# Two w_ada sections side by side: 512-wide adds on DVE, a quarter of the rows streamed through PE, rotary angles on POOL

## The chip, the cores and the metric

The kernel runs on one core of a Trainium2 chip. The metric is the device time of one execution in microseconds; shorter is better. Before the change it is 2480.28 us, the median of three runs (2477.94 to 2485.64).

The core's engines run side by side, each working through its own queue in order: PE (matrix multiply), DVE (vector), ACT (activation), POOL (GpSimd) and SP, which here only issues DMA transfers. An instruction that must wait holds up everything behind it in its engine's queue.

## The reference

One decoder block on x of 512 tokens by 2048 channels. A vector c gives six modulation vectors, and the first two of them (shift1, scale1) are needed before anything else can be projected:

```
mod = silu(c) @ w_ada + b_ada          # w_ada 2048 x 12288; six sections of 2048 columns
sh1, sc1, g1, sh2, sc2, g2 = split(mod)
u   = rmsnorm(x) * (1 + sc1) + sh1
z   = u @ w_in                         # q, k, v of two head groups, gates
y   = concat(rmsnorm(forgetting attention), rmsnorm(sparse attention)) @ w_out
h   = x + g1 * y
h   = h + g2 * swiglu(rmsnorm(h) * (1 + sc2) + sh2)
out = rmsnorm(h)
```

The sparse attention rotates q and k by cos and sin of position times frequency; the kernel makes these two tables itself.

## The kernel before, in words

Activations are held transposed, channels on the partitions: 16 chunks of 128 channels by 512 tokens. Every product with a weight is done in three passes of reduced-precision fp32r matmuls (high x high, low x high, high x low). For that each weight tile is split: ACT casts the high part `wh`, and DVE or POOL subtracts it to leave the low part `wl` (`fetch_w`, L218 to L243). `u` is split in the same way (`modulate_a` and `modulate_b`, L383 to L393: `mt` on DVE, `uh` on ACT, `ul` on DVE).

The change sits in the first stage, the loop of L474 to L545. It streams the first two sections of `w_ada` (scale1 and shift1, 33.5 MB), forms `silu(c) @ w_ada` as it goes, and feeds the first projections as soon as two chunks of `u` are known. It is written out by hand as steps; the order of the instructions in each queue is the order in which the steps emit them.

- A block `j` is 256 columns of both sections; there are `NJ` = 8 blocks of 8 steps. Each step loads one `w_ada` tile of 512 KB. The tiles go round in a ring of 8 buffers (tag `adw`), which the tiles of x, loaded first, use too.
- A tile before holds four row groups of 128 rows by 256 columns of one section. One step later, the row groups are multiplied with their scalar of `sl` (silu of c) and summed: DVE adds two or three of the four into `acc` (L492, L494); for the others ACT multiplies into `tm` (L499, L502) and POOL adds into `acc2` (L503).
- When a block is through (`due`, with the lags of `LAGS`), PE sums both accumulators over the partitions with a column of ones (L511), DVE adds the bias (L520) and makes `mt`, `uh` follows on ACT, and `ul` on DVE one step later.
- The two new chunks of `u` then release matmul units (`units`, L447), which are queued in `todo`; each step takes two of them, or three in the second half. A unit is three matmuls of 128x128 by 512. `S0` holds four banks for the query projection (first half) and then the compress inputs (second half), `S1` three banks for keys.
- The weights of these units are loaded in step 2 of each block (`w_pairs`, L437) and split one block later, in steps 0, 2 and 4 (L536 to L542): number 0 is the query or a compress tile, number 1 the key tile, number 2 (second half only) another compress tile. POOL makes the low parts; DVE makes that of number 1 in the second half.
- The rotary angles are a generator (`tables`, L397). From step 6 on it yields one DVE instruction per step (L543), 24 in all, and at its end two Sin passes on ACT.

After the loop, the key banks are rotated and the next projection begins (`z_qn`, L694).

The lines that the steps of the prediction touch:

```
due: step == n + LAGS[n == SLOTS - 1][what]        # LAGS = (3, 4, 5), (2, 3, 4)
units: for k in range(2) for m in range(len(outs)) # 8 units for S0, 6 for S1
for _ in range(2 if step < 8 * HJ + LAGS[0][2] else 3): todo.pop(0)()
```

Of the kernel before, what the change touches and what calls it, by code (L numbers as in the profile page):

```python
# [26 lines left out]
ADW = 8  # L27
# [50 lines left out]
def hymba_block(ctx: ExitStack, tc: tile.TileContext, x, c, positions, w_ada, b_ada, norm_attn,  # L78
                norm_ffn, w_in, b_fgate, cmp_pos, w_kc1, w_kc2, w_vc1, w_vc2, beta_fox, beta_nsa,
                w_out, w_gate, w_up, w_down, final_norm, cst, out):  # L80
    nc = tc.nc
    x, out = x[0], out[0]
    w_ada, w_in, w_out = w_ada[0], w_in[0], w_out[0]
# [25 lines left out]
    def bank(tag, shape=(P, T)):  # L109
        return ps.tile(list(shape), F32, tag=tag, name=uid("ps" + tag), bufs=SETS[tag])  # L110
# [16 lines left out]
    xtok = {}  # L127
    for t in range(NT):
        for g in range(2):
            xt = early.tile([P, D // 2], F32, tag="adw", name=uid("xtok"), bufs=ADW)  # L130
            nc.sync.dma_start(xt, x[t * P:(t + 1) * P, g * 1024:(g + 1) * 1024])
            xtok[t, g] = xt
    rows1 = early.tile([P, P], F32, name="rows1")
    nc.gpsimd.dma_start(rows1[0:96], b_ada.rearrange("o (r p) -> (o r) p", p=P))
# [7 lines left out]
    posi = early.tile([P, T], I32, name="posi")  # L142
# [4 lines left out]
    sl = con.tile([P, ND], F32, name="sl")  # L147
    se = con.tile([P, ND], F32, name="se")
    b = bank("o")
# [31 lines left out]
    tags = BANKS_A + BANKS_B  # L181
    for t in range(NT):
        for g in range(4):
            src = xtok[t, g // 2][:, g % 2 * T:(g % 2 + 1) * T]
            b = bank(tags[(t * 4 + g) % 8], (P, 4, P))
            for i in range(4):
                nc.tensor.transpose(b[:, i, :], src[:, i * P:(i + 1) * P], ident)
            dst = xT[:, 4 * g:4 * g + 4, t * P:(t + 1) * P]
            junk = early.tile([P, T], F32, tag="mt", name=uid("junk"), bufs=2)
            if g % 2 == 0:  # L190
                nc.scalar.activation(junk, src, AF.Square, accum_out=ssq4[:, t, g:g + 1])
                nc.vector.tensor_copy(dst, b)
            else:
                nc.vector.scalar_tensor_tensor(junk, src, 1.0, src, op0=OP.mult, op1=OP.mult,
                                               accum_out=ssq4[:, t, g:g + 1])
                nc.scalar.copy(dst, b)
    nc.vector.tensor_reduce(ssq, ssq4, axis=AX.X, op=OP.add)
    vec = con.tile([P, P + 64], F32, name="vec")
    b = bank("s")
    nc.tensor.transpose(b[:, 0:P], rows1, ident)  # L200
    nc.vector.tensor_copy(vec[:, 0:P], b[:, 0:P])
    b = bank("s")
# [192 lines left out]
    cosT = sinT = None  # L395

    def tables():  # L397
        nonlocal cosT, sinT
        cosT = wts.tile([P, T], F32, tag="cos", name="cosT")
        sinT = wts.tile([P, T], F32, tag="sin", name="sinT")  # L400
        ang = posi.bitcast(F32)
        nc.vector.tensor_copy(ang, posi)
        yield
        nc.vector.tensor_scalar(ang, ang, cs[:, K_FRQ:K_FRQ + 1], None, op0=OP.mult)
        yield
        for dst, turn in ((sinT, 0.0), (cosT, 0.25)):
            kk = mid.tile([P, T], F32, tag="wx", name=uid("kk"))
            nc.vector.tensor_scalar(kk, ang, 1.0 / TWO_PI, turn, op0=OP.mult, op1=OP.add)
            yield
            nc.vector.tensor_scalar(kk, kk, MAGIC, None, op0=OP.add)  # L410
            yield
            nc.vector.tensor_scalar(kk, kk, MAGIC, None, op0=OP.subtract)
            yield
            cur = ang
            for pc in _pi_parts():
                nc.vector.scalar_tensor_tensor(dst, kk, -pc, cur, op0=OP.mult, op1=OP.add)
                cur = dst
                yield
            if turn:
                nc.vector.tensor_scalar(dst, dst, TWO_PI / 4, None, op0=OP.add)  # L420
                yield
            nc.vector.tensor_scalar(dst, dst, PI_C, -PI_C, op0=OP.min, op1=OP.max)
            yield
        for dst in (sinT, cosT):
            nc.scalar.activation(dst, dst, AF.Sin)

    S0 = [bank(t) for t in BANKS_B]
    S1 = [bank("mm") for _ in range(3)]
# [6 lines left out]
    HJ = NJ // 2  # L435
# [25 lines left out]
    SLOTS = 8 * NJ  # L461
# [3 lines left out]
            if step == n + LAGS[n == SLOTS - 1][what]:  # L465
                return n

    def on_dve(n):
        return n % 2 == 0

    tiles, accs, accs2, sums, halves, fetched, todo = {}, {}, {}, {}, {}, {}, []
    extra_work = tables()
    step = 0
    while step < SLOTS + 8 or todo:  # L474
        j, r = divmod(step, 8)
        if j < NJ:
            sec, q0 = (1, 0)[r // 4], 4 * (r % 4)
            tiles[step] = early.tile([P, 4, 256], F32, tag="adw", name=uid("ad"), bufs=ADW)
            c0 = sec * D + j * 256
            nc.sync.dma_start(tiles[step], w_ada[:, c0:c0 + 256].rearrange("(q p) n -> p q n", p=P)[:, q0:q0 + 4, :])  # L480
        if r == 2 and j < NJ:
            fetched[j] = w_pairs(j)
        n = step - 1
        if 0 <= n < SLOTS:
            key, q0 = n // 4, 4 * (n % 4)
            if q0 == 0:
                accs[key] = early.tile([P, 256], F32, tag="acc", name=uid("acc"), bufs=3)
            acc = accs[key]
            for q in (0, 1, 3) if on_dve(n) else (0, 1):
                sc1 = sl[:, q0 + q:q0 + q + 1]  # L490
                if q0 + q == 0:
                    nc.vector.tensor_scalar(acc, tiles[n][:, q, :], sc1, None, op0=OP.mult)  # L492
                else:
                    nc.vector.scalar_tensor_tensor(acc, tiles[n][:, q, :], sc1, acc, op0=OP.mult, op1=OP.add)  # L494
            for q in (2,) if on_dve(n) else (2, 3):
                sc1 = sl[:, q0 + q:q0 + q + 1]
                if q0 + q == 2:
                    accs2[key] = early.tile([P, 256], F32, tag="acc2", name=uid("acc2"), bufs=3)
                    nc.scalar.activation(accs2[key], tiles[n][:, q, :], AF.Copy, scale=sc1)  # L499
                else:  # L500
                    tm = early.tile([P, 256], F32, tag="tm", name=uid("tm"), bufs=2)
                    nc.scalar.activation(tm, tiles[n][:, q, :], AF.Copy, scale=sc1)  # L502
                    nc.gpsimd.tensor_tensor(accs2[key], accs2[key], tm, op=OP.add)  # L503
        n = due(step, 0)
        if n is not None:
            jj = n // 8
            sums[jj] = bank("mm")
            for k2 in range(2):
                for av in (accs, accs2):
                    for i in range(2):  # L510
                        nc.tensor.matmul(sums[jj][:, 2 * k2 + i:2 * k2 + i + 1],  # L511
                                         av[2 * jj + k2][:, i * P:(i + 1) * P], one_col,
                                         start=k2 == 0 and av is accs and i == 0,
                                         stop=av is accs2, skip_group_check=True)
        n = due(step, 1)
        if n is not None:
            jj = n // 8
            for k2, sec in ((0, 1), (1, 0)):
                m0 = sec * ND + 2 * jj
                nc.vector.tensor_tensor(mod[:, m0:m0 + 2], sums[jj][:, 2 * k2:2 * k2 + 2], b_mod[:, m0:m0 + 2],  # L520
                                        op=OP.add)
            scale_vec(0, jj * 2, 2)
            pend = [modulate_a(0, i, xT[:, i, :], rstd1, early) for i in (2 * jj, 2 * jj + 1)]
        n = due(step, 2)
        if n is not None:
            u.extend([modulate_b(*h) for h in pend])
            jj = n // 8
            if jj < HJ:
                todo += units(halves[jj][0], jj, S0, ND // 2)
            if jj == HJ - 1:  # L530
                todo.append(keep_half)
            todo += units(halves[jj][1], jj, S1, ND)
        for _ in range(2 if step < 8 * HJ + LAGS[0][2] else 3):
            if todo:
                todo.pop(0)()
        if 0 < j <= NJ and r % 2 == 0 and r // 2 < len(fetched[j - 1]):  # L536
            i = r // 2
            w = fetched[j - 1][i](nc.vector if i == 1 and j > HJ else nc.gpsimd)
            halves.setdefault(j - 1, []).append(w)
            pr = 2 * (j - 1 - HJ) + i // 2  # L540
            if j > HJ and i != 1:
                todo += units(w, pr, S0, ND)  # L542
        if step >= 6:  # L543
            next(extra_work, None)
        step += 1  # L545
    for i in range(ND):
        nc.sync.dma_start(xsp[i], xT[:, i, :])
# [176 lines left out]
    b = bank("s")  # L724
    for t in range(NT):
        nc.tensor.matmul(b[0:8, t * P:], lf[:, t, :], tri[:, 0:T - t * P],
                         start=t == 0, stop=t == NT - 1)
# [196 lines left out]
    for pr in range(4):  # L924
# [4 lines left out]
        for i in range(2):  # L929
            q = pair("q", 6, "qf")  # L930
# [243 lines left out]
    kk = ExitStack()  # L1174
# [173 lines left out]
```

## Time and profile before

| | us |
|---|---|
| median of three runs | 2480.28 |
| the profiled execution | 2482.39 |
| its span in the trace | 2480.6 |
| PE busy | 2345.2 (95%) |
| DVE busy | 1626.7 (66%) |
| ACT busy | 1053.7 (42%) |
| POOL busy | 451.3 (18%) |

A trace row gives start, duration, engine, line, operation, the names of output and inputs and their shapes; in brackets stands how long the engine was idle before and what ended that. Matmuls overlap, so their pace is read from the distance of their starts. An fp32 matmul leaves two records, an fp32r matmul one. The granted clock of PE is a share of its full 2.4 GHz; it is at 1.00 or at 0.50 (1.2 GHz), and a stretch between has some of both.

### The profile page before, as it was taken

How to read it: one execution, taken by the hardware profiler on the slowest of the kernel's cores; microseconds unless marked ns; L12 is line 12 of the kernel's file. 1: busy time of each engine (PE TensorE's matmuls, PEld its weight loads, DVE VectorE, ACT ScalarE, POOL GpSimd, SP SyncE). 2: the span in 40 equal slices, each digit the busy share in tenths (PEclk: the TensorE clock that was granted, in tenths of full speed). 3: DMA queues.
4: the chain of work that ended last, by engine and by line, in shares of the span. 5: the costliest groups of instructions: out<-in, count | busy, mean ns of one | idle time of the engine just before them, and what ended most of it. 6: DMA issues, size and time to landing. Idle time of an engine off the chain costs nothing.

```text
span 2480.6 us, 38623 instructions
## 1 busy us (share of the span) xinstructions
PE 2345.2 (95%) x14659; PEld 2100.3 (85%) x14659; DVE 1626.7 (66%) x2757; ACT 1053.7 (42%) x1618; POOL 451.3 (18%) x466
## 2 busy tenths in 40 slices
PE   4688999999999989979999999999999899999998
PEld 3567888787887867779999999999999888888887
DVE  8995787877756566497677777777776633333333
ACT  4343543433423332255555555555555422222233
POOL 5564000200010221152121212121222100000011
PEclk7799999999999999989999999999999999999999
DMA  9783644444646257838988899888988654333322
GB/s 300 238 265 89 196 139 143 124 132 124 181 142 188 73 186 251 257 90 216 225 220 222 220 222 229 223 216 221 224 193 202 179 171 134 125 119 123 102 94 102
DMA packets 321690, 440.31 MB, mean 178 GB/s; under 512 B 25200, under 2 KB 216528, under 8 KB 321504
## 3 DMA queue, kind: packets, MB, share of 16 engines
q1 hardware_dynamic: 288080, 348.20, 43.6%
q0 software_dynamic: 31120, 85.45, 18.5%
q10 hardware_dynamic: 2304, 4.20, 0.4%
q8 instruction: 115, 1.88, 0.3%
q14 instruction: 71, 0.58, 0.1%
HBM read 340.18 MB, written 28.38 MB: 149 GB/s over the span
## 4 chain that ended last, share of the span: by engine, by line
PE 53%; DVE 1%; issue 0%; ACT 0%; DMA 0%; SPq 0%; DVEq 0%; ACTq 0%
PE py L1105 11%; PE py L1108 11%; PE py L1107 11%; PE psmm L255 3%; PE psmm L257 3%; PE psmm L256 3%; PE pss L255 2%; PE pss L256 2%; PE pss L257 2%; PE pso L257 1%; PE pso L256 1%; PE pso L255 1%; PE pso L1005 0%; DVE ul L1088 0%; DVE ls L1054 0%
## 5 line engine op out<-in xcount | busy, mean ns | idle before, releaser
L240 DVE TENSOR_TENSOR wl<-wr,wh 128x1024 fp32r<-128x1024 f32 (+2 forms) x194 | 218.5, 1126 | 359.6 <-ACT wh L239 358.0
L239 ACT CAST wh<-wr 128x1024 fp32r<-128x1024 f32 (+2 forms) x210 | 199.0, 948 | 498.1 <-PE psmm L256 205.5
L1108 PE MATMUL py<-uh,ls 128*128 128x256 f32 x1408 | 398.4, 283 | 3.7 <-DVE ls L1054 3.7
L1105 PE MATMUL py<-uh,hs 128*128 128x256 f32 x1408 | 399.4, 284 | 0.9 <-DVE ev L1122 0.5
L1107 PE MATMUL py<-ul,hs 128*128 128x256 f32 x1408 | 397.5, 282 | 2.5 <-DVE ul L1088 2.5
L1048 ACT CAST hs<-sum 128x1024 fp32r<-128x1024 f32 x176 | 184.7, 1049 | 379.6 <-PE py L1107 255.0
L1054 DVE TENSOR_TENSOR ls<-sum,hs 128x1024 fp32r<-128x1024 f32 x176 | 215.4, 1224 | 194.5 <-ACT hs L1048 194.5
L1107 PE MATMUL py<-ul,hx 128*128 128x256 f32 x1056 | 299.3, 283 | 4.0 <-DVE ul L1088 4.0
L1105 PE MATMUL py<-uh,hx 128*128 128x256 f32 x1056 | 299.0, 283 | 1.7 <-ACT uh L1087 1.4
L1108 PE MATMUL py<-uh,lx 128*128 128x256 f32 x1056 | 299.1, 283 | 0.0
L1108 PEld LDWEIGHTS py<-uh,ls 128*128 128x128 f32 x1408 | 266.8, 189 | 4.8 <-DVE ls L1054 4.7
L1107 PEld LDWEIGHTS py<-ul,hs 128*128 128x128 f32 x1408 | 266.7, 189 | 3.8 <-DVE ul L1088 3.8
L1105 PEld LDWEIGHTS py<-uh,hs 128*128 128x128 f32 x1408 | 267.5, 190 | 2.6 <-DVE ev L1122 1.3
L1044 POOL DMA_DIRECT2D lx<-raw x176 | 155.8, 885 | 592.5 <-ACT lx L1043 432.8
L1107 PEld LDWEIGHTS py<-ul,hx 128*128 128x128 f32 x1056 | 200.2, 190 | 5.3 <-DVE ul L1088 5.3
L1105 PEld LDWEIGHTS py<-uh,hx 128*128 128x128 f32 x1056 | 200.6, 190 | 2.2 <-ACT uh L1087 1.7
L1108 PEld LDWEIGHTS py<-uh,lx 128*128 128x128 f32 x1056 | 200.3, 190 | 0.0
L358 DVE SCALAR_TENSOR_TENSOR acc<-ad,sl,acc 128x512 f32<-128x512 f32 x180 | 143.0, 794 | 47.6 <-DMA ad<-in_w_ada_dram 45.9
L1043 ACT ACTIVATE lx<-raw 128x768 fp32r<-128x768 f32 x176 | 147.9, 840 | 1.8 <-DMA raw<-in_w_gate_dram 1.8
L1039 ACT CAST hx<-raw 128x768 fp32r<-128x768 f32 x176 | 144.3, 820 | 5.5 <-DMA raw<-in_w_gate_dram 5.5
L255 PE MATMUL psmm<-fh,wh 128*128 128x512 f32 x352 | 137.0, 389 | 0.0
L257 PE MATMUL psmm<-fh,wl 128*128 128x512 f32 x352 | 136.9, 389 | 0.0
(440 smaller groups left out, 5480.9 us busy)
## 6 DMA issues: line engine op xcount, KB each, us to landing
ad<-in_w_ada_dram SPq DMA_DIRECT2D x192, 512.0 KB, 4.6
lx<-raw POOLq DMA_DIRECT2D x176, 384.0 KB, 5.1
raw<-in_w_up_dram SPq DMA_DIRECT2D x176, 256.0 KB, 4.1
raw<-in_w_gate_dram SPq DMA_DIRECT2D x176, 256.0 KB, 4.5
wr<-in_w_down_dram SPq DMA_DIRECT2D x88, 512.0 KB, 3.6
wr<-in_w_in_dram SPq DMA_DIRECT2D x104, 256.0 KB, 3.5
wr<-in_w_in_dram SPq DMA_DIRECT2D x24, 512.0 KB, 4.4
wr<-in_w_out_dram SPq DMA_DIRECT2D x24, 512.0 KB, 5.1
```

What stands on the lines that cost most here:

```text
L239: nc.scalar.copy(wh[:, :, s], v)
L240: lo.tensor_tensor(wl[:, :, s], v, split_ap(wh)[:, :, s], op=OP.subtract)
L255: nc.tensor.matmul(dst, wh[:, k, w], ah, start=first, stop=False)
L256: nc.tensor.matmul(dst, wh[:, k, w], al, start=False, stop=False)
L257: nc.tensor.matmul(dst, wl[:, k, w], ah, start=False, stop=last)
L1043: nc.scalar.activation(lx[s], raw[s][:, 1:4, :], AF.Copy, scale=-1.0)
L1044: nc.gpsimd.dma_start(split_ap(lx[s]), raw[s][:, 1:4, :], accum_op=OP.add)
L1048: nc.scalar.copy(hs[s], sums[s])
L1054: nc.vector.tensor_tensor(ls[s], sums[s], split_ap(hs[s]), op=OP.subtract)
L1105: nc.tensor.matmul(o, wh[:, wi, js], vh[:, vi, :], start=k == 0 and j == 0, stop=False, skip_group_check=True)
L1107: nc.tensor.matmul(o, wh[:, wi, js], vl[:, vi, :], start=False, stop=False, skip_group_check=True)
L1108: nc.tensor.matmul(o, wl[:, wi, js], vh[:, vi, :], start=False, stop=k == KG - 1, skip_group_check=True)
```

## The change

A `w_ada` tile now holds two row groups of 128 rows by 512 columns: 256 of the scale section beside 256 of the shift section, brought by two transfers of 256 KB. A step therefore has two 512-wide row groups in place of four 256-wide ones. DVE adds both into `acc`, except in the steps that `on_pe` names (steps 0 to 6 of block 0, steps 3 to 6 of the others): there DVE adds the first, and one step later PE streams the second as an fp32 matmul, with the scalar broadcast to 128x128 as its weights, into one bank `rows`. After the last of these in a block, ACT copies one row of the bank (`row`). The sum over partitions takes this row and `acc`. ACT and POOL no longer multiply and add row groups.

The rotary angles go to POOL, all at once and ahead of the loop; ACT converts the positions for them, and the Sin passes stand at step 12. What was one fused instruction per part of 2 pi is now a multiplication and an addition. The low part of weight number 1 is made by DVE in all blocks. The tiles of x, which share the ring, change shape but not content.

```diff
+        ts, tt = nc.gpsimd.tensor_scalar, nc.gpsimd.tensor_tensor
         ang = posi.bitcast(F32)
-        nc.vector.tensor_copy(ang, posi)
-        yield
-        nc.vector.tensor_scalar(ang, ang, cs[:, K_FRQ:K_FRQ + 1], None, op0=OP.mult)
-        yield
+        nc.scalar.copy(ang, posi)
+        ts(ang, ang, cs[:, K_FRQ:K_FRQ + 1], None, op0=OP.mult)
+        kk = mid.tile([P, 2, T], F32, tag="wx", name=uid("kk"))
+        kt = kk[:, 1, :]
+        kk = kk[:, 0, :]
         for dst, turn in ((sinT, 0.0), (cosT, 0.25)):
...
+            ts(kk, ang, 1.0 / TWO_PI, turn, op0=OP.mult, op1=OP.add)
+            ts(kk, kk, MAGIC, None, op0=OP.add)
+            ts(kk, kk, MAGIC, None, op0=OP.subtract)
             cur = ang
             for pc in _pi_parts():
-                nc.vector.scalar_tensor_tensor(dst, kk, -pc, cur, op0=OP.mult, op1=OP.add)
+                ts(kt, kk, -pc, None, op0=OP.mult)
+                tt(dst, cur, kt, op=OP.add)
                 cur = dst
...
+                ts(dst, dst, TWO_PI / 4, None, op0=OP.add)
+            ts(dst, dst, PI_C, -PI_C, op0=OP.min, op1=OP.max)
...
-    def on_dve(n):
-        return n % 2 == 0
+    def on_pe(n):
+        j, r = divmod(n, 8)
+        return r < 7 if j == 0 else 3 <= r < 7
...
-    extra_work = tables()
+    tables()
...
-            sec, q0 = (1, 0)[r // 4], 4 * (r % 4)
-            tiles[step] = early.tile([P, 4, 256], F32, tag="adw", name=uid("ad"), bufs=ADW)
-            c0 = sec * D + j * 256
-            nc.sync.dma_start(tiles[step], w_ada[:, c0:c0 + 256].rearrange("(q p) n -> p q n", p=P)[:, q0:q0 + 4, :])
+            tiles[step] = early.tile([P, 2, T], F32, tag="adw", name=uid("ad"), bufs=ADW)
+            for i, sec in ((0, 1), (1, 0)):
+                c0 = sec * D + j * 256
+                nc.sync.dma_start(tiles[step][:, :, i * 256:(i + 1) * 256],
+                                  w_ada[:, c0:c0 + 256].rearrange("(q p) n -> p q n", p=P)[:, 2 * r:2 * r + 2, :])
...
-            for q in (0, 1, 3) if on_dve(n) else (0, 1):
+            for q in range(1 if on_pe(n) else 2):
...
-            for q in (2,) if on_dve(n) else (2, 3):
...
-                    nc.scalar.activation(tm, tiles[n][:, q, :], AF.Copy, scale=sc1)
-                    nc.gpsimd.tensor_tensor(accs2[key], accs2[key], tm, op=OP.add)
+        n = step - 2
+        if 0 <= n < SLOTS and on_pe(n):
+            jj, q = n // 8, 2 * (n % 8) + 1
+            first = n == 0 or not on_pe(n - 1)
+            if first:
+                rows[jj] = bank("mm")
+            nc.tensor.matmul(rows[jj], sl[:, q:q + 1].to_broadcast([P, P]), tiles[n][:, 1, :],
+                             start=first, stop=not on_pe(n + 1))
+            if not on_pe(n + 1):
+                row = early.tile([1, T], F32, tag="row", name=uid("row"), bufs=2)
+                nc.scalar.copy(row, rows[jj][0:1, :])
+                rows[jj] = row
...
+            for av, one in ((rows.pop(jj), one_col[0:1, :]), (accs.pop(jj), one_col)):
+                for i in range(4):
+                    nc.tensor.matmul(sums[jj][:, i:i + 1], av[:, i * P:(i + 1) * P], one,
+                                     start=one is not one_col and i == 0, stop=one is one_col,
+                                     skip_group_check=True)
...
-            w = fetched[j - 1][i](nc.vector if i == 1 and j > HJ else nc.gpsimd)
+            w = fetched[j - 1][i](nc.vector if i == 1 else nc.gpsimd)
...
-        if step >= 6:
-            next(extra_work, None)
+        if step == 12:
+            for dst in (sinT, cosT):
+                nc.scalar.activation(dst, dst, AF.Sin)
```

## Rows read from the trace of the kernel before

**Rows 1.** Busy us per stretch, PE, PEld, DVE, ACT, POOL, clock, DMA share, GB/s.

```profile
20.00:40.00 20.00, 4.32 (x17) 3.85 (x18) 18.01 (x34) 11.14 (x22) 12.86 (x14) 0.54 1.10 351
40.00:60.00 20.00, 11.48 (x38) 9.05 (x39) 19.57 (x28) 8.00 (x15) 12.30 (x11) 0.60 0.83 273
...
120.00:140.00 20.00, 18.70 (x86) 14.73 (x85) 19.45 (x30) 9.94 (x19) 10.18 (x12) 0.98 0.58 185
...
160.00:180.00 20.00, 17.16 (x82) 13.73 (x80) 19.41 (x26) 7.83 (x15) 12.78 (x12) 1.00 0.80 255
```

**Rows 2.** Waits of the DMA queue to 211 us: total, times, longest.

```profile
SPq L480 <- DVE acc L494: 61.9, 33, 5.5
```

**Rows 3.** DVE in order of time, from 20 us: start, duration.

```profile
22.72 3.61 DVE L494 SCALAR_TENSOR_TENSOR acc<-ad,sl,acc 128x256 f32<-128x256 f32 x7
```

**Rows 4.** Groups by line to 300 us: busy and mean, idle before.

```profile
L494 DVE SCALAR_TENSOR_TENSOR acc<-ad,sl,acc 128x256 f32<-128x256 f32 x144 | 111.1, 772 | 4.8 <-DMA ad<-in_w_ada_dram 0.6
...
L392 DVE SCALAR_TENSOR_TENSOR ul<-mt,mod,uh 128x512 fp32r<-128x512 f32 x16 | 17.7, 1146 | 0.0
```

**Rows 5.** PE in order of time, around the loop's end.

```profile
205.90 0.39 PE L255 MATMUL pss<-uh,wh 128*128 128x512 f32 x1
...
211.15 0.39 PE L257 MATMUL pso<-uh,wl 128*128 128x512 f32 x1
214.80 0.50 PE L255 MATMUL psmm<-uh,wh 128*128 128x512 f32 x1 [3.27 <-ACT wh L239]
```

**Rows 6.** DVE in order of time, 40 to 52 us.

```profile
43.36 0.42 DVE L410 TENSOR_SCALAR kk<-kk 128x512 f32<-128x512 f32 x1
...
46.39 0.22 DVE L520 TENSOR_TENSOR mod<-psmm,vec 128x2 f32<-128x2 f32 x2
...
46.85 1.41 DVE L386 SCALAR_TENSOR_TENSOR mt<-xT,a_vec,rstd 128x512 f32<-128x512 f32 x2
48.18 0.68 DVE L416 SCALAR_TENSOR_TENSOR sinT<-kk,posi 128x512 f32<-128x512 f32 x1
...
51.97 1.21 DVE L416 SCALAR_TENSOR_TENSOR sinT<-kk,sinT 128x512 f32<-128x512 f32 x1
```

**Rows 7.** The page's costliest groups.

```profile
L358 DVE SCALAR_TENSOR_TENSOR acc<-ad,sl,acc 128x512 f32<-128x512 f32 x180 | 143.0, 794 | 47.6 <-DMA ad<-in_w_ada_dram 45.9
```

**Rows 8.** The DMA queue's issues in order of time.

```profile
1.65 5.22 SPq L131 DMA_DIRECT2D xtok<-in_x_dram  x8
```

**Rows 9.** PE in order of time, fp32 matmuls: 172 us and 312 us.

```profile
172.47 1.84 PE L511 MATMUL psmm<-cs,acc 128*128 128x1 f32 x16
...
312.76 1.02 PE L726 MATMUL pss<-tri,lf 128*8 128x512 f32 x2
```

**Rows 10.** ACT in order of time, from 19 us.

```profile
24.59 0.59 ACT L175 COPY rstd<-psmm 128x512 f32<-128x512 f32 x1 [3.04 <-PE psmm L173]
```

**Rows 11.** POOL's groups by line and shape, whole span.

```profile
L503 POOL TENSOR_TENSOR acc<-acc,tm 128x256 f32<-128x256 f32 x80 | 68.5, 859 | 82.1 <-ACT tm L502 78.1
L240 POOL TENSOR_TENSOR wl<-wr,wh 128x1024 fp32r<-128x1024 f32 x12 | 31.3, 2608 | 6.8 <-ACT wh L239 6.8
L571 POOL TENSOR_TENSOR r<-r,sw 128x512 f32<-128x512 f32 x12 | 18.8, 1569 | 1.7 <-DVE r L569 0.8
...
L570 POOL TENSOR_TENSOR sw<-sw,sinT 128x512 f32<-128x512 f32 x12 | 16.2, 1348 | 88.6 <-ACT sw L568 65.7 <-DVE part L690 22.9
```

**Rows 12.** PE in order of time, the loop's first units.

```profile
50.97 0.80 PE L256 MATMUL pss<-ul,wh 128*128 128x512 f32 x1 [1.76 <-DVE ul L392]
...
55.83 0.41 PE L255 MATMUL pss<-uh,wh 128*128 128x512 f32 x1
```

**Rows 13.** A compress tile's cast on ACT, then PE's wait for it.

```profile
166.87 1.04 ACT L239 CAST wh<-wr 128x1024 fp32r<-128x1024 f32 x1
...
170.75 0.50 PE L257 MATMUL pss<-uh,wl 128*128 128x512 f32 x1 [0.94 <-POOL wl L240]
```

**Rows 14.** Busy us per stretch, columns as in group 1: a fall of the clock.

```profile
182.00:184.00 2.00, 2.00 (x6) 1.55 (x5) 1.97 (x3) 1.40 (x4) 2.00 (x2) 0.53 1.06 407
```

More of the change, by code (lines that the diff above doesn't have):

```diff
@@ L129, in hymba_block @@
         for g in range(2):
-            xt = early.tile([P, D // 2], F32, tag="adw", name=uid("xtok"), bufs=ADW)
-            nc.sync.dma_start(xt, x[t * P:(t + 1) * P, g * 1024:(g + 1) * 1024])
+            xt = early.tile([P, 2, T], F32, tag="adw", name=uid("xtok"), bufs=ADW)
+            nc.sync.dma_start(xt, x[t * P:(t + 1) * P, g * 1024:(g + 1) * 1024].rearrange("p (a b) -> p a b", b=T))
             xtok[t, g] = xt
@@ L183, in hymba_block @@
         for g in range(4):
-            src = xtok[t, g // 2][:, g % 2 * T:(g % 2 + 1) * T]
+            src = xtok[t, g // 2][:, g % 2, :]
             b = bank(tags[(t * 4 + g) % 8], (P, 4, P))
@@ L400, in tables @@
         sinT = wts.tile([P, T], F32, tag="sin", name="sinT")
+        ts, tt = nc.gpsimd.tensor_scalar, nc.gpsimd.tensor_tensor
         ang = posi.bitcast(F32)
-        nc.vector.tensor_copy(ang, posi)
-        yield
-        nc.vector.tensor_scalar(ang, ang, cs[:, K_FRQ:K_FRQ + 1], None, op0=OP.mult)
-        yield
-        for dst, turn in ((sinT, 0.0), (cosT, 0.25)):
[L407 to L413, printed above, removed]
+        nc.scalar.copy(ang, posi)
[3 more added lines that the diff above has]
+        kk = kk[:, 0, :]
+        for dst, turn in ((sinT, 0.0), (cosT, 0.25)):
+            ts(kk, ang, 1.0 / TWO_PI, turn, op0=OP.mult, op1=OP.add)
+            ts(kk, kk, MAGIC, None, op0=OP.add)
+            ts(kk, kk, MAGIC, None, op0=OP.subtract)
             cur = ang
             for pc in _pi_parts():
-                nc.vector.scalar_tensor_tensor(dst, kk, -pc, cur, op0=OP.mult, op1=OP.add)
+                ts(kt, kk, -pc, None, op0=OP.mult)
+                tt(dst, cur, kt, op=OP.add)
                 cur = dst
-                yield
             if turn:
[L420 to L425, printed above, removed]
+                ts(dst, dst, TWO_PI / 4, None, op0=OP.add)
+            ts(dst, dst, PI_C, -PI_C, op0=OP.min, op1=OP.max)
     S0 = [bank(t) for t in BANKS_B]
@@ L466, in due @@
                 return n
-    def on_dve(n):
-        return n % 2 == 0
-    tiles, accs, accs2, sums, halves, fetched, todo = {}, {}, {}, {}, {}, {}, []
-    extra_work = tables()
+    def on_pe(n):
+        j, r = divmod(n, 8)
+        return r < 7 if j == 0 else 3 <= r < 7
+    tiles, accs, rows, sums, halves, fetched, todo = {}, {}, {}, {}, {}, {}, []
+    tables()
     step = 0
@@ L484, in hymba_block @@
         if 0 <= n < SLOTS:
-            key, q0 = n // 4, 4 * (n % 4)
+            jj, q0 = n // 8, 2 * (n % 8)
             if q0 == 0:
-                accs[key] = early.tile([P, 256], F32, tag="acc", name=uid("acc"), bufs=3)
-            acc = accs[key]
-            for q in (0, 1, 3) if on_dve(n) else (0, 1):
+                accs[jj] = early.tile([P, T], F32, tag="acc", name=uid("acc"), bufs=2)
+            acc = accs[jj]
+            for q in range(1 if on_pe(n) else 2):
                 sc1 = sl[:, q0 + q:q0 + q + 1]
@@ L494, in hymba_block @@
                     nc.vector.scalar_tensor_tensor(acc, tiles[n][:, q, :], sc1, acc, op0=OP.mult, op1=OP.add)
-            for q in (2,) if on_dve(n) else (2, 3):
[L496 to L501, printed above, removed]
-                    nc.scalar.activation(tm, tiles[n][:, q, :], AF.Copy, scale=sc1)
-                    nc.gpsimd.tensor_tensor(accs2[key], accs2[key], tm, op=OP.add)
+        n = step - 2
[10 more added lines that the diff above has]
+                rows[jj] = row
         n = due(step, 0)
@@ L507, in hymba_block @@
             sums[jj] = bank("mm")
[L508 to L514, printed above, removed]
+            for av, one in ((rows.pop(jj), one_col[0:1, :]), (accs.pop(jj), one_col)):
[3 more added lines that the diff above has]
+                                     skip_group_check=True)
         n = due(step, 1)
```

## The prediction

> **What bounds the kernel now.** I read the page's engine shares first, and they put PE in front; but a share is a mean over stages, and the change touches only the first one. So I cut that stage into stretches of 20 us next. From 40 to 180 us DVE is busy over 19.4 us of every 20 (three of these seven stretches stand in the rows), while PE has 11 to 19, at granted clocks from 0.60 up to 1.00, and DMA falls from 351 GB/s to between 185 and 273 [rows 1]. The waits of the DMA queue say why it falls: 61.9 us in total for DVE's adds to free a tile [rows 2]. So DVE bounds the stage up to the last add. Its adds of 128x256 take 0.52 us each while POOL has nothing to do (seven in 3.61 us) [rows 3]; their mean over the stage is 0.77, x144 [rows 4]. Last I looked for where the stage hands over: the loop's last matmul starts at 211.15 and streams 0.23 us, so the loop ends on PE at 211.4; PE then stands until ACT has cast the next weight [rows 5]. What follows hangs on that end in the same way after the change, so I carry a shift of it through one to one.
>
> **What the change takes away.** DVE loses 160 adds of 256 columns and the 24 angle instructions, and gets 93 adds of 512. A 512-wide instruction with two tensors takes 0.68 us without POOL and 1.21 beside it [rows 6]; later in this kernel the same add has a mean of 0.79 [rows 7]. Per column block (8 steps) DVE then has 12 x 0.79 = 9.5, 1.9 for mod, scale and mt [rows 6], two ul of 1.15 [rows 4] and one weight subtraction, priced like an ul. That is 14.8 us; now 20 adds at 0.77 are 15.4 by themselves, with the rest and the angles beside them. DVE stops being the bound. The ACT and POOL adds go too, but neither engine was the bound, so I count nothing for them. The doubled number of w_ada transfers moves the same bytes in the same 1 KB runs; 20 issues per block at 0.65 us (eight in 5.22) [rows 8] are 13 us on the queue, under the pace found below: nothing.
>
> **What is late next: PE.** At full clock 23 matmuls start between 205.90 and 211.15, 0.228 us each [rows 5]. The loop has 432 of them: 18 per block for S1 (8 blocks), 24 for each of four first-half weight tiles, 24 for each of eight compress tiles. New are 35 fp32 matmuls of 512 columns. The trace has this form once: two records per matmul, the second 0.43 us after the first, so 0.86 us [rows 9]. Seven of them (block 0) run early, while PE has nothing else; 28 stand in PE's queue between the units. The column sums stay at 16 records per block, 1.84 us [rows 9].
>
> When can PE begin? Its first unit needs the low part of the first weight tile, which POOL subtracts, and all 26 angle instructions are now ahead of it in POOL's queue. They begin when ACT has converted the positions, behind the copy of rstd, which ends at 25.2 [rows 10]; plus 0.6 for a pass of 512 columns, 25.8. Eight of the 26 have two inputs: 1.35 and 1.57 us, mean 1.46, for 512 columns, 0.86 for 256 [rows 11]. The other 18 have one tensor input, and the trace has no such instruction on POOL. The two-input rows give 2.35 ns per column and 0.26 us fixed; half the slope gives 0.26 + 0.60 = 0.86. The ends: 0.42, what DVE takes for it [rows 6], and 1.57, the dearer two-input row. I take 0.86, as POOL must fetch half as much. Angles: 18 x 0.86 + 8 x 1.46 = 27.2, to 53.0; then the subtraction, 2.6 [rows 11]: PE starts in earnest at 55.6 (47.7 to 68.4). Before, its units ran on from 51.0 [rows 12], so they start later. ACT also stands in this time, since Sin waits for the angles; queued behind it are weight casts and a row copy needed only some 10 us later. The tiles come in meanwhile (19 of them and the weights are 18 MB, 52 us at 351 GB/s [rows 1]), so the DMA loses little.
>
> From there PE has 430 x 0.228 = 98.0, 28 x 0.86 = 24.1 and 7 x 1.84 = 12.9: 135.0 us. To this come its waits:
> - Blocks 1 to 3: from the column sums to the first ul. The rows have 46.39 for mod and 48.26 for the end of mt [rows 6], 1.87; one 512-wide add and one ul at 0.68 make 3.3, with the hand-over 3.4. Two units and one matmul (1.6) lie beside it: 1.8 each, 5.4. Later blocks have five units there: nothing.
> - Second half, a new wait: the row copy on ACT waits for the last streamed matmul of the block, and the cast of the next compress tile is queued behind it, then POOL's subtraction. 0.2 + 0.55 + 1.04 + 2.6 = 4.4 us [rows 10, 11, 13], beside two units and two matmuls (1.8): 2.5 in two blocks, 1.1 and 0.6 where more units lie between: 6.7. Before, this wait cost 0.94 [rows 13].
> - Clock: after a stand PE's matmuls came 0.43 us apart from 50.97 to 55.83, where the lower level ended [rows 12]; the same at the start here costs 2.5. One fall later, as from 182 (0.53 over 2 us) [rows 14], costs 0.9, and the two microseconds behind it as much again: 1.8.
>
> Sum: 55.6 + 135.0 + 5.4 + 6.7 + 2.5 + 1.8 = 207.0, against 211.4: 4.4 us less. By blocks: one of the first half has 42 x 0.228 + 3.4 + 1.8 + 1.8 = 16.6 us, one of the second 66 x 0.228 + 3.4 + 1.8 + 2.5 = 22.7; before, the loop took 160.4 from 51.0 on, 20 a block. The gain is made in the first half, and much of it is given back by the late start and in the second. The profiled execution took 2482.39 (span 2480.6), so 2478.0; it lay 2.1 above the median 2480.28, so against that 2475.9.
>
> In the Trainium skill, GPSIMD Engine Reference, section 4.1 Engine selection, POOL is about twice as slow as VectorE on two inputs and roughly at line rate on one. The trace agrees for two inputs (1.46 against 0.68); no run here shows one input. With one input at DVE's plain 0.68, the angles would end 3.2 us sooner and the time would be 2472.7.
>
> **Rivals.**
> 1. *PE's new waits stay hidden* (chance 0.31). The second half's 6.7 shrinks to the 0.9 per block seen before [rows 13], 3.6; the clock never falls again (1.8); one-input passes take 0.6, towards their lower end (4.7 off). 207.0 - 3.1 - 1.8 - 4.7 = 197.4: 2466. For it: the clock stayed at 0.98 and 1.00 in the later stretches though PE waited in each [rows 1]. Against: the row copy is ahead of the cast in ACT's queue.
> 2. *The stage falls to the DMA's pace* (0.07). 47 MB at 351 GB/s are 134 us, the last tile at 137; the last add stood 18 us before the loop's end, so about 160 and 2430. For it: the queue's waits [rows 2]. Against: the 135 us of PE work cannot begin at 25 us, and PE does not skip any of it.
> 3. *POOL's angles hold up the first units: slower* (0.21). One place: the first low part behind 26 instructions. If a one-input pass costs as much as the dearest two-input one, 1.57 [rows 11], the angles take 40.8 us with all 26 at that price, PE starts at 69.2, and the loop ends at 220.6: 9.2 us more, 2489.5. It decides from about 1.5 us per one-input pass. For it: these were 24 instructions of 0.42 to 1.21 us on DVE where rows show them [rows 6] and POOL has no row for them. Against: the read of one tensor less. The same page of the Trainium skill, in its opening, calls POOL the wrong choice for ordinary elementwise work, which speaks for this rival.
> 4. *The change doesn't do what it says* (part of the forecast): DVE is freed, but the time turns into PE's.
>
> **How the numbers follow.** A measurement of this kernel tells about 0.3%, 7.4 us, from no change. Forecast, -4.4 us: no change, chance 0.41; its own range is 2472 to 2483. Faster is rivals 1 and 2, 0.38. Slower is rival 3, 0.21. The unknown costs reach from -21 (one-input passes at 0.42, no new waits) to +19 (at 1.57, with two more falls of the clock and twice the new waits). I leave out rival 2 and the outer part of the others: 2462 to 2489.
>
> **What would show it.** PE's first unit with a low part near 55.6, right behind POOL's last angle and one subtraction; POOL's one-input passes near 0.86; streamed matmuls at 0.43 per record; DVE at about 65% from 60 to 200 us and waiting for PE's sums; PE busy over 90% there; in the second half PE waiting 2 to 3 us per block for a low part from POOL; the loop's last matmul near 207. A loop that ends before 200 or after 215 makes the prediction wrong, as would DMA at 350 GB/s throughout.

## The result, and the profile after

The changed kernel takes 2494.41 us, median of four runs (2491.69 to 2494.76), against 2480.07 for four of the kernel before (2477.94 to 2485.64). The ratio is 1.0052, with a 95% interval of 1.0034 to 1.0070. So it is slower, by some 13 us, and the interval leaves out no change; 2475.9 was predicted (range 2462 to 2489). The profiled executions took 2491.69 (span 2489.9) and 2482.39 (span 2480.6).

The stretches of [rows 1] and the one from 60 to 80 us, in the kernel after (same columns):

```profile
20.00:40.00 20.00, 13.36 (x40) 7.96 (x39) 14.31 (x25) 5.40 (x8) 12.93 (x9) 0.73 1.09 351
40.00:60.00 20.00, 1.59 (x2) 0.57 (x2) 19.09 (x21) 3.36 (x4) 18.98 (x13) 0.50 0.69 220
60.00:80.00 20.00, 11.92 (x34) 7.95 (x35) 0.00 (x0) 1.15 (x3) 7.68 (x6) 0.66 0.26 79
...
120.00:140.00 20.00, 17.06 (x66) 11.67 (x66) 13.77 (x21) 3.36 (x6) 2.25 (x1) 0.91 0.47 146
...
160.00:180.00 20.00, 18.08 (x81) 13.18 (x79) 12.67 (x16) 4.58 (x6) 5.26 (x2) 1.00 0.70 227
```

DVE is no longer the bound: from 120 to 140 and from 160 to 180 us it is busy 13 to 14 us of 20, where it had 19.4 in [rows 1]. But from 40 to 60 us PE does next to nothing, and from 60 to 80 DVE does nothing at all and the DMA moves 79 GB/s. POOL alone is full, up to 66 us. PE in order of time shows what that does to the loop's start and end (it answers to [rows 5, 12]; in brackets the idle time before and what ended it):

```profile
49.22 0.80 PE L256 MATMUL pss<-ul,wh 128*128 128x512 f32 x1 [1.14 <-DVE ul L392]
68.08 0.80 PE L257 MATMUL pss<-uh,wl 128*128 128x512 f32 x1 [18.06 <-POOL wl L240]
...
229.68 0.39 PE L257 MATMUL pso<-uh,wl 128*128 128x512 f32 x1
233.19 0.50 PE L255 MATMUL psmm<-uh,wh 128*128 128x512 f32 x1 [3.12 <-ACT wh L239]
```

The first low part comes at 68.08 instead of the 55.6 predicted, and the loop's last matmul at 229.68 instead of 207 (211.15 in [rows 5]): 18.5 us later than before. POOL's groups from 25 to 66 us, by shape (busy us, mean ns), say why the start is late:

```profile
L414 POOL TENSOR_SCALAR kk<-kk 128x512 f32<-128x512 f32 x8 | 13.9, 1735 | 0.7
L415 POOL TENSOR_TENSOR sinT<-sinT,kk 128x512 f32<-128x512 f32 x3 | 4.3, 1430 | 0.2
...
L410 POOL TENSOR_SCALAR kk<-kk 128x512 f32<-128x512 f32 x2 | 3.3, 1650 | 0.2
...
L409 POOL TENSOR_SCALAR kk<-posi 128x512 f32<-128x512 f32 x2 | 1.6, 816 | 0.2
...
L419 POOL TENSOR_SCALAR cosT<-cosT 128x512 f32<-128x512 f32 x1 | 0.6, 613 | 0.1
```

The passes with one operation (L410, L411, L414, L418) cost more than the two-input adds (L415); those with two operations (L409, L419) cost about half as much as the adds.

The rest of the loss is inside the loop. ACT's Sin, which waited for POOL's angles, was over at 66.4; what follows repeats in every later block. One block's hand-over, ACT and DVE first, then PE, 96 to 108 us:

```profile
97.92 0.57 ACT L501 COPY row<-psmm 1x512 f32<-1x512 f32 x1 [9.73 <-PE psmm L497]
98.41 1.78 ACT L239 CAST wh<-wr 128x1024 fp32r<-128x1024 f32 x2
...
100.22 2.49 DVE L240 TENSOR_TENSOR wl<-wr,wh 128x768 fp32r<-128x768 f32 x1 [4.22 <-ACT wh L239]
102.63 1.52 DVE L490 SCALAR_TENSOR_TENSOR acc<-ad,sl,acc 128x512 f32<-128x512 f32 x2
104.07 0.22 DVE L517 TENSOR_TENSOR mod<-psmm,vec 128x2 f32<-128x2 f32 x2
...
96.81 1.02 PE L497 MATMUL psmm<-ad,sl 128*128 128x512 f32 x2
...
97.90 0.40 PE L256 MATMUL psmm<-ul,wh 128*128 128x512 f32 x1
...
106.01 0.50 PE L255 MATMUL pss<-uh,wh 128*128 128x512 f32 x1 [1.91 <-ACT uh L388]
107.25 0.50 PE L256 MATMUL pss<-ul,wh 128*128 128x512 f32 x1 [0.73 <-DVE ul L392]
```

ACT waits for PE's last streamed matmul (L497) to copy its row; both casts are queued behind the copy; DVE's queue stands before the low part of the second weight, and behind that stand two adds of the next block, and then `mod` and `mt`. PE's sums over the partitions are over before (they start at 100.56). Only then comes `uh` on ACT, for which PE waits. So PE's own stream decides when PE gets its next `u`. I call this the tie. DVE's waits from 40 to 200 us (total, times, longest) sum it up:

```profile
DVE wl L240 <- ACT wh L239: 43.2, 6, 22.4
```

The longest is the stand at the start, 59.4 to 81.8 us. It has two parts, as ACT and then DVE show in order of time:

```profile
65.75 0.63 ACT L542 ACTIVATE cosT<-cosT 128x512 f32<-128x512 f32 x1 [15.56 <-POOL cosT L419]
79.48 0.57 ACT L501 COPY row<-psmm 1x512 f32<-1x512 f32 x1 [13.10 <-PE psmm L497]
81.77 2.50 DVE L240 TENSOR_TENSOR wl<-wr,wh 128x768 fp32r<-128x768 f32 x1 [22.36 <-ACT wh L239]
```

For the first 7 us ACT's queue stands in Sin for POOL. After that it stands 13.1 us in front of the row copy, while PE, late, works through the units queued ahead of its streamed matmuls. So the tie already makes the larger part of this stand; the other five waits, 20.8 us, are the tie alone.

### The profile page after: what moved, and what is told of

Read it like the earlier page. It is cut to its first block, busy times and chain, and to the rows that moved or that the text cites. A ratio compares the mean times of both kernels' runs of the same rounds, so it can differ in the third digit from the quotient of the medians.

```text
span 2489.9 us, 38545 instructions
## 1 busy us (share of the span) xinstructions
PE 2361.6 (95%) x14729; PEld 2099.8 (84%) x14729; DVE 1579.6 (63%) x2675; ACT 1015.7 (41%) x1531; POOL 407.9 (16%) x408
## 4 chain that ended last, share of the span: by engine, by line
PE 53%; DVE 1%; issue 1%; ACT 0%; DMA 0%; SPq 0%; DVEq 0%; ACTq 0%
PE py L1103 11%; PE py L1106 11%; PE py L1105 11%; PE psmm L257 3%; PE psmm L255 3%; PE psmm L256 3%; PE pss L255 2%; PE pss L257 2%; PE pss L256 2%; PE pso L257 1%; PE pso L256 1%; PE pso L255 1%; PE pso L1003 0%; DVE ul L1086 0%; DMA out_dram<-ot 0%
## 5 line engine op out<-in xcount | busy, mean ns | idle before, releaser
L240 DVE TENSOR_TENSOR wl<-wr,wh 128x1024 fp32r<-128x1024 f32 (+2 forms) x198 | 231.9, 1171 | 394.9 <-ACT wh L239 392.8
```

What stands on the lines that cost most here:

```text
L240: lo.tensor_tensor(wl[:, :, s], v, split_ap(wh)[:, :, s], op=OP.subtract)
```

## The experiments

Two theories at the start. A: the late start is the cause, made by the price of POOL's one-operation passes ahead of the first low part. B: PE is the bound, by the streamed matmuls and by waits for a cast behind the row copy, and the late start is absorbed. From the second set on, C: the tie, which turns an earlier start into longer waits; against D: the tiles (DVE's adds, the DMA) hold an early PE.

Ratios are against the kernel before, timed on the same chip. Its median was 2480.07 beside the kernel after, 2483.76 beside e1 to e4, 2482.18 beside f1 to f4 and 2484.11 beside g1 to g4; these differ by up to 0.16%, so smaller differences between ratios of two sets say nothing. "Loop end" is the start of the loop's last matmul, and the loop is counted from the first low part on PE; both are from one profiled execution of each kernel.

| kernel | first low part | loop end | PE idle in the loop | granted clock in the loop | ratio (95%) |
|---|---|---|---|---|---|
| before | 51.6 | 211.2 | 29.4 | 0.88 | 1 |
| after | 68.1 | 229.7 | 13.0 | 0.95 | 1.0052 (1.0034 to 1.0070) |
| e1 two operations | 60.0 | 226.3 | 15.8 | 0.94 | 1.0041 (1.0028 to 1.0054) |
| e2 late angles | 48.4 | 233.4 | 21.9 | 0.87 | 1.0023 (1.0009 to 1.0037) |
| e3 no stream | 68.4 | 207.9 | 21.0 | 0.92 | 0.9971 (0.9960 to 0.9982) |
| e4 cast first | 68.9 | 215.1 | 3.7 | 0.98 | 1.0006 (0.9995 to 1.0016) |
| f1 late, cast first | 46.8 | 196.8 | 5.5 | 0.96 | 0.9923 (0.9908 to 0.9939) |
| f2 f1, fewer streamed | 46.5 | 196.9 | 9.0 | 0.87 | 0.9928 (0.9913 to 0.9942) |
| f3 late, no stream | 48.9 | 199.9 | 30.3 | 0.89 | 0.9943 (0.9928 to 0.9959) |
| f4 f3, two edits more | 49.7 | 203.0 | 29.9 | 0.87 | 0.9950 (0.9935 to 0.9966) |
| g1 e1 and e4 | 60.0 | 206.3 | 3.7 | 0.98 | 0.9962 (0.9948 to 0.9975) |
| g2 f1, two operations | 46.9 | 196.7 | 5.4 | 0.96 | 0.9935 (0.9911 to 0.9959) |
| g3 f1, mixed | 46.2 | 193.0 | 7.0 | 0.95 | 0.9914 (0.9896 to 0.9932) |
| g4 f1, angles on DVE | 45.5 | 199.3 | 5.6 | 0.94 | 0.9921 (0.9900 to 0.9942) |

**e1: two operations per pass on POOL.**

```diff
-            ts(kk, kk, MAGIC, None, op0=OP.add)
+            ts(kk, kk, 1.0, MAGIC, op0=OP.mult, op1=OP.add)
...
-                ts(kt, kk, -pc, None, op0=OP.mult)
+                ts(kt, kk, -pc, 0.0, op0=OP.mult, op1=OP.add)
...
```

> The 13 POOL passes that have one operation and an immediate (1.49 to 2.08 us each in the changed kernel) are written with two operations (times 1.0, or plus 0.0), as the form of L409 that took 0.69 and 0.94; nothing else changes. Theory A (the late start of PE, made by the price of the one-operation passes): 13 x about 0.85 us go, POOL's angles end near 55 instead of 65.7, the first low part is there near 57 and PE's first unit with it stands near 57 instead of 68; the time falls by about 11 us, to 2483. Theory B (PE is the bound by the streamed matmuls and the waits for a cast behind the row copy; the late start is absorbed): the passes may get cheaper, but the time stays within 4 us of 2494.

POOL's groups of this kernel, as above, and the first low part on PE:

```profile
L414 POOL TENSOR_SCALAR kk<-kk 128x512 f32<-128x512 f32 x8 | 7.4, 928 | 0.7
...
L404 POOL TENSOR_SCALAR posi<-posi,cs 128x512 f32<-128x512 f32 x1 | 1.6, 1573 | 19.9 <-ACT posi L403 19.9
...
L410 POOL TENSOR_SCALAR kk<-kk 128x512 f32<-128x512 f32 x2 | 1.6, 776 | 0.2
```

```profile
59.98 0.79 PE L257 MATMUL pss<-uh,wl 128*128 128x512 f32 x1 [8.80 <-POOL wl L240]
```

The same arithmetic with a second, empty operation takes 0.93 us instead of 1.74; L404, left with one operation, still takes 1.57. So the form sets the price. PE starts 8 us earlier, yet the loop ends only 3.4 us earlier and the time is 2494.24: the same. Theory B was right that the time would not move, but the reason is in the next runs.

**e2: late angles.** The angles, in the changed kernel's forms, become a generator again, one POOL instruction per step from step 8 on, with Sin at its end.

```diff
-    tables()
+    extra_work = tables()
...
+        if step >= 8:
+            next(extra_work, None)
```

> The angles stay on POOL in the same forms, but are issued one per step from step 8 on, behind the first weight's low part in POOL's queue, with Sin at the end. Theory A: PE's first unit waits only for the first modulated tile and stands near 50 instead of 68; the loop ends near 212 instead of 230 and the time falls by about 18 us, to 2476, near the kernel before. Theory B: PE begins earlier but has the same 135 us of work and the same waits, and is overtaken by the tiles' arrival; the loop ends no more than 6 us earlier, the time is 2488 or above.

PE in order of time, around the starts of three blocks, then the whole loop with its granted clock (third from the right), then DVE's waits:

```profile
47.78 0.79 PE L256 MATMUL pss<-ul,wh 128*128 128x512 f32 x1 [1.80 <-DVE ul L392]
48.37 0.63 PE L257 MATMUL pss<-uh,wl 128*128 128x512 f32 x1
...
69.04 0.50 PE L255 MATMUL pss<-uh,wh 128*128 128x512 f32 x1 [3.13 <-ACT uh L388]
71.63 0.80 PE L256 MATMUL pss<-ul,wh 128*128 128x512 f32 x1 [2.10 <-DVE ul L392]
...
92.27 0.49 PE L255 MATMUL pss<-uh,wh 128*128 128x512 f32 x1 [2.50 <-ACT uh L388]
94.87 0.79 PE L256 MATMUL pss<-ul,wh 128*128 128x512 f32 x1 [2.10 <-DVE ul L392]
```

```profile
48.37:233.63 185.26, 163.38 (x599) 118.04 (x597) 114.88 (x142) 37.17 (x51) 62.52 (x34) 0.87 0.63 203
```

```profile
DVE wl L240 <- ACT wh L239: 33.6, 6, 9.8
```

PE starts 20 us earlier than after, and the loop ends no earlier. DVE waits 33.6 us for casts, now all through the loop. PE waits 4.3 to 5.2 us at each start of blocks 1 to 3 (the rows show the first two of these), and after the wait at 71.63 its matmuls come back 0.43 us apart instead of 0.23: a mean granted clock of 0.87, between the levels of 1.2 and 2.4 GHz, costs 0.13 x 185 = 24 us of the loop. The median, 2489.03 (2483.34 to 2501.90; the profiled execution is the slowest of these), is 5.4 us under the kernel after. Theory A's 18 us did not come; what B named "the same waits" did, but they grew.

**e3: no streamed matmuls after block 0.**

```diff
-        return r < 7 if j == 0 else 3 <= r < 7
+        return j == 0 and r < 7
...
```

> The 28 streamed fp32 matmuls of blocks 1 to 7 go back to DVE as 28 more adds of 512 columns (and with them the row copies and the first four column sums of these blocks); block 0 and the angles stay as they are. Theory B (PE bound by them): 28 x 0.86 = 24 us of PE and about 9 us of waits behind the row copy go; the loop's end falls from 230 to about 200, the time to about 2462. Theory A (late start): PE still begins at 68; DVE then has 16 x 0.79 + 5.3 = 18 us per block, under what the second half of PE needs, so what PE gains is about 8 to 12 us; the time is about 2483.

```profile
80.00:100.00 20.00, 14.39 (x57) 10.67 (x55) 19.50 (x28) 4.29 (x6) 2.57 (x1) 0.91 0.61 194
```

The time is 2477.50, between the two theories. The loop ends 21.8 us earlier than after, where B had 30, but the first low part stays at 68.36, and DVE is the bound again, with 19.50 of 20 us in this stretch. A and B each hold a part of the cost. With the streamed matmuls the row copies went too, and with them the tie: DVE's stand for the cast at the start is 4.42 us here, where after has 22.36, though the angles are as early and as slow.

**e4: the cast ahead of the row copy.** Only the place where ACT's copy is issued moves, behind the casts of the same step.

```diff
-            if not on_pe(n + 1):
-                row = early.tile([1, T], F32, tag="row", name=uid("row"), bufs=2)
-                nc.scalar.copy(row, rows[jj][0:1, :])
-                rows[jj] = row
...
+        n = step - 2
+        if 0 <= n < SLOTS and on_pe(n) and not on_pe(n + 1):
+            jj = n // 8
+            row = early.tile([1, T], F32, tag="row", name=uid("row"), bufs=2)
+            nc.scalar.copy(row, rows[jj][0:1, :])
+            rows[jj] = row
```

> Only ACT's order changes: the copy of the streamed row is issued behind the cast of the next block's first weight instead of ahead of it. Theory B: the second half's wait for POOL's low part (0.9 to 2.4 us per block on PE) goes and the time falls by about 6 us, to 2488; the rows of PE show no wait for POOL there. Theory A: the waits may go, but the time stays within 3 us of 2494, and PE's first unit with a low part stays at 68.

The same hand-over as shown above of after (ACT, DVE, PE), the whole loop, and DVE's waits:

```profile
96.18 0.58 ACT L540 COPY row<-psmm 1x512 f32<-1x512 f32 x1 [8.80 <-PE psmm L497]
96.66 0.83 ACT L239 CAST wh<-wr 128x768 fp32r<-128x768 f32 x1
...
97.52 0.96 DVE L240 TENSOR_TENSOR wl<-wr,wh 128x768 fp32r<-128x768 f32 x1 [1.15 <-ACT wh L239]
...
102.83 0.50 PE L255 MATMUL pss<-uh,wh 128*128 128x512 f32 x1 [0.48 <-ACT uh L388]
104.07 0.50 PE L256 MATMUL pss<-ul,wh 128*128 128x512 f32 x1 [0.74 <-DVE ul L392]
```

```profile
68.94:215.28 146.34, 142.69 (x598) 105.41 (x598) 100.52 (x132) 33.86 (x47) 32.30 (x14) 0.98 0.76 246
```

```profile
DVE wl L240 <- ACT wh L239: 29.0, 5, 21.8
```

Behind the copy now stands one cast instead of two, POOL's subtraction no longer falls beside DVE's, and DVE's low part takes 0.96 us, where it took 2.49 with POOL's subtraction beside it (99.53 to 101.89). Apart from the stand at the start DVE waits 7.2 us for casts instead of 20.8, PE is idle 3.7 us instead of 13.0, and the loop is 15.4 us shorter. The time is 2486.67, level with the kernel before and 7.7 us under after: a little more than B's 6 us, and not only in the second half. The stand at the start stays (21.8 us), since the second cast is still behind the copy there.

**f1 to f4: both causes taken away.** f1 is e2 and e4 together. f2 adds `5 <= r < 7` for `3 <= r < 7`, f3 is e2 and e3 together, f4 is f3 with the forms of e1 and the first half's second low part on POOL.

> Both edits of e2_late (angles one per step behind the first weight) and e4_cast_first (row copy behind the cast). Theory C (the row copy ties ACT, DVE and PE together: PE's last streamed matmul, the copy, the cast, DVE's low part, DVE's last adds, the sums, the next modulated tile; an early PE only waits longer there and comes back at the lower clock): with the tie cut the early start counts; PE's first low part near 48, the loop about 147 us long as in e4_cast_first (146.1), its end near 196 and the time about 17 us under e4_cast_first, 2470. Theory D (an early PE is held by the tiles: DVE's adds beside POOL's angles, or the DMA): PE waits 3 us or more per block for the modulated tile as in e2_late, the loop ends at 208 or later, the time is 2482 or more.

> f1_late_cast with two streamed matmuls per block instead of four in blocks 1 to 7: 14 x 0.86 = 12 us less on PE, 14 adds of 512 columns more on DVE. Theory C with PE as the bound: the loop ends 8 to 12 us before that of f1_late_cast, the time is near 2460. Theory D: DVE is the bound once PE starts early, the loop ends at the time of f1_late_cast or later.

> Late angles of e2_late and no streamed matmuls in blocks 1 to 7 as in e3_no_stream, so no row copy ahead of a cast either. Theory A/C: the stand of DVE and PE up to 68 us goes, the loop ends 15 us or more before that of e3_no_stream (207.9), near 192, the time is 2463. Theory D: DVE, at 19.5 of 20 us in e3_no_stream and slower beside POOL's angles, is the bound; the loop ends near 203, the time is 2473.

> f3_late_nostream with the two-operation forms of e1_two_op and the low part of the second weight on POOL in the first half, as in the kernel before. If DVE is the bound in f3_late_nostream, its 2.5 us per first-half block count: the loop ends 5 to 10 us earlier, the time is 4 to 10 us under f3_late_nostream. If PE is, the time is the same within 3 us.

The whole loop of f1 and DVE's waits in it:

```profile
46.80:197.07 150.27, 144.76 (x599) 106.65 (x597) 118.57 (x142) 36.19 (x50) 62.17 (x33) 0.96 0.78 253
```

```profile
DVE wl L240 <- ACT wh L239: 7.9, 4, 2.8
```

f1 is as theory C has it: the loop ends at 196.8 and the time is 2463.61 (expected 196 and 2470). By the medians late angles alone brought 5.4 us and the cast alone 7.7 (0.29% and 0.46% by the ratios); together they bring 30.8 (1.29%), because the early start counts only once the tie is cut. Theory D's waits are small.

f2 sheds 12 us of PE's work and ends at the same time. Stretches of f2, then of f1:

```profile
60.00:80.00 20.00, 16.68 (x61) 11.90 (x60) 19.61 (x24) 3.63 (x5) 14.03 (x9) 0.74 0.83 260
80.00:100.00 20.00, 16.31 (x59) 11.57 (x60) 19.61 (x24) 3.63 (x5) 9.49 (x6) 0.74 0.87 274
```

```profile
60.00:80.00 20.00, 18.78 (x87) 13.63 (x86) 19.39 (x23) 3.63 (x5) 15.21 (x9) 1.00 0.93 292
80.00:100.00 20.00, 16.92 (x65) 11.58 (x64) 17.29 (x23) 3.63 (x5) 9.17 (x6) 0.91 0.89 281
```

With DVE full and PE waiting a little more, the granted clock is 0.74 where f1 has 1.00 and 0.91. Over the loop 0.87 of 150.6 us loses 19.6 us, against 6.0 (0.96 of 150.3) in f1: in size, what PE sheds comes back as clock. That does not make the clock the cause: in these stretches DVE is full, as theory D has it, and PE may only be slow in the time that DVE leaves it. No run separates the two. f3 takes 2469.35 and ends its loop at 199.9, between its theories (2463 and 2473); with no streamed work PE is idle 30.3 us, and DVE is the bound. f4, 2471.55, was to be 4 to 10 us under f3 and is not; it has two edits, so it says only that they bring nothing together.

**g1 to g4.** g1 is e1 and e4 together, g2 is f1 with e1's forms, g3 keeps four streamed matmuls in blocks 1 to 3 and two in blocks 4 to 7, and g4 is f1 with the angles on DVE as in the kernel before.

> Both edits of e1_two_op (two-operation forms on POOL, angles still first) and e4_cast_first. By itself the cheaper form moved PE's first low part from 68.1 to 60.0 and the time not at all. Theory C (what PE wins at the start is lost to the tie through the row copy, not to the angles): with the tie cut the loop is 146 us long from 60.0, ends near 206, and the time is about 8 us under that of e4_cast_first, 2478. If C is wrong and an earlier PE always waits longer, the loop ends near 215 and the time is that of e4_cast_first, 2486.

> f1_late_cast with the two-operation forms. If POOL's passes slow DVE's adds beside them (1.2 us beside POOL, 0.79 without), 11 us less of POOL work from 27 to 110 us lets DVE deliver the first blocks sooner; PE's idle falls from 5.5 to about 3 us, the loop ends 3 to 6 us earlier, the time is 2459. If PE alone sets the loop (135 of its 150 us are its work), the time is the same within 3 us, 2463.

> f1_late_cast with two streamed matmuls per block instead of four in blocks 4 to 7 only, where PE is busy without a break: 8 x 0.86 = 6.9 us less on PE. If PE's work sets the second half, the loop ends near 190 and the time is 2457. If, as in f2_late_cast_few, what PE sheds comes back as stretches at a lower granted clock, the loop ends within 2 us of 196.8 and the time is 2463.

> f1_late_cast with the angles on DVE, in the form and at the steps of the kernel before: the move to POOL is undone, the streamed matmuls and the cast ahead of the row copy stay. If the move is worth something, DVE's 24 instructions (0.4 to 1.2 us each, about 18 us) hold up the first three blocks, where DVE is busy 19.5 of 20 us in f1_late_cast; the loop ends 6 to 15 us later, 2470 to 2478. If POOL's angles beside DVE cost its adds as much as they save, the time is the same within 3 us, 2463, or less.

g1 ends its loop at 206.3, as C expected, and takes 2474.08: the cheaper form, which brought nothing clear of noise with the tie (2494.24 against 2494.41), brings 0.44% without it (1.0006 to 0.9962). g2 takes 2467.97 (ratio 0.9935, 0.9911 to 0.9959; loop end 196.7), the same as f1. g3's loop ends 3.8 us earlier than f1's, half of what it sheds; its 2461.75 is the lowest median here, and not apart from f1's by the intervals. g4 takes 2463.73, the same as f1. DVE's adds and `ul` from 25 to 120 us (busy, mean ns), first of f1, then of g4, show why the place of the angles does not matter there:

```profile
L501 DVE SCALAR_TENSOR_TENSOR acc<-ad,sl,acc 128x512 f32<-128x512 f32 x56 | 61.4, 1097 | 4.5 <-DMA ad<-in_w_ada_dram 3.2
L392 DVE SCALAR_TENSOR_TENSOR ul<-mt,mod,uh 128x512 fp32r<-128x512 f32 x8 | 6.0, 787 | 0.0
```

```profile
L496 DVE SCALAR_TENSOR_TENSOR acc<-ad,sl,acc 128x512 f32<-128x512 f32 x55 | 47.0, 854 | 4.5 <-DMA ad<-in_w_ada_dram 3.4
L392 DVE SCALAR_TENSOR_TENSOR ul<-mt,mod,uh 128x512 fp32r<-128x512 f32 x8 | 9.9, 1277 | 0.0
```

Beside POOL's angles an add takes 0.24 us more on the mean. Over 56 adds that is 14 us. Against it stand the angle instructions, which take DVE 10 us in g4, and `ul`, which takes 4 us more there. (The angles on DVE are 19 instructions in the traces of before and g4; the 24 given ahead of the experiments is a miscount.)

So, with both causes gone, the gain over the kernel before does not come from moving the angles (g4 against f1). Nor does it rest on the streamed matmuls of blocks 1 to 7: f3, without them, has 0.9943 against f1's 0.9923, and the intervals overlap. The 512-wide adds in place of those of ACT and POOL are the main part left; no run tests them by themselves.

## Why the prediction was wrong

- **The step that failed first** is the term 18 x 0.86, the one-input passes on POOL. It priced a pass by how many tensors it reads; the trace prices it by its form. Fourteen passes with one operation took 1.67 us on the mean (23.4 us; single ones 1.49 to 2.08), four with two operations 0.71, and the eight two-input adds 1.39 against 1.46 predicted. With some 2 us between instructions the angles took 39.4 us instead of 27.2, and the first low part came 12.5 us late. e1 shows by itself that the form is the cause of the price. The upper bound, 1.57 [rows 11], was close; the choice went by a slope that the form overrules. The Trainium skill (GPSIMD Engine Reference, section 4.1 Engine selection) has one input at roughly line rate, which leans the same way. Measured against DVE's 0.42 [rows 6], a pass with two operations at 0.61 comes near it and one with one operation at 1.49 does not (both with DVE idle, 60 to 66 us); the measurement decides.
- **The second** is "queued behind it are weight casts and a row copy needed only some 10 us later", and that the DMA loses little. DVE's next low part was behind those casts, so DVE stood 22.4 us (7 for Sin, 13.1 for the row copy, the rest for copy and casts), SP stood up to 22.6 us in front of tiles, and the DMA fell to 79 GB/s.
- **The third** is the place of the row copy. I saw that it is ahead of the cast in ACT's queue and priced it where PE waits for POOL's low part in the second half, 6.7 us (measured 4.9: 0.88, twice 1.70, and small ones). I did not follow it to DVE, in whose queue a low part now stands in every block: at the starts of blocks 1 to 3 PE waits 8.2 us, where 5.4 were put down. PE's idle of 13.0 us in all is close to the 12.1 predicted, but its consequence was not priced: 0.05 of 161.8 us, 8 us, lost to the clock, where 4.3 were put down. e4 shows what the tie was worth: 15.4 us of loop.
- **Right**: DVE stops being the bound, PE becomes it, and a streamed matmul costs PE the 0.86 us predicted (from 96.81 to 97.90 lie one of them and one matmul of 0.23). PE's work comes out some 5 us above the predicted 135: loop less idle less clock is 161.8 - 13.0 - 8.1 = 140.7, and 139.7 in e4. Where these 5 us lie is open.
- **The sum again**: the loop ends at 229.9 (its last matmul's start and 0.23), 22.9 us after the 207.0 predicted. Of these 12.5 are the late start, 5.7 PE's work, 3.8 the clock and 0.9 the waits. So the price of POOL's passes is the largest error, and the tie shows little in this sum only because most of its wait had been put down, at another place.
- **The carry "one to one"** holds only roughly: the loop ends 18.5 us later and the median is 14.3 higher, the profiled execution 9.3 higher. The later stages vary by themselves (the kernel before took 2477.06 to 2493.41 beside these experiments), so a single profile bears a shift out to within some 9 us.
- **Rival 3 came true** in place and sign: 69.2 forecast for the first low part, 68.08 measured; the 18 passes took 1.46 us on the mean, about its point of 1.5. It gave 2489.5, and the median is 5 us above that, with the tie. It had a chance of 0.21, on the argument that reading one tensor less must be cheaper, for which no row spoke.

## What to carry to other kernels

When a step is moved, follow every queue from its new place to all that stands behind it, through each engine, back to the one that feeds it: a small copy that waits for the last matmul of a block can hold up the casts for the next. Two causes in series hide each other, so an edit that does little alone may be half of the gain; try them together before dropping one. Work taken from one engine may come back as a lower granted clock there (f2) or as slower instructions on a neighbour (the angles beside DVE's adds).

## What the runs showed of the hardware

- On POOL, 128x512 fp32 with an immediate: 1.49 to 2.08 us with one operation, 0.61 to 0.94 with two (in e1 once 1.17 and once 1.21), with an add, an empty add or a max as the second; 1.57 for one operation with a per-partition scalar.
- DVE's 128x768 subtraction took 0.96 us by itself and 2.49 beside POOL's 128x1024 one; its 512-wide add 0.75 by itself and 1.6 beside POOL's subtraction and angles (five in 8.02 from 46.74 us in f1).
- Less work on PE, with a little more waiting, left its time the same: granted clock 0.87 against 0.96 (f2, f1).
